# A pair's accumulators summed in mid-pair, the recurrence's elementwise work issued over three chunks, and the last two gate blocks made plain

## The chip, the cores and the metric

The kernel runs on one core of a Trainium2 chip. The metric is the time of one execution in device microseconds; it is given as the median of three runs. A profile is one execution taken by the hardware profiler, and its times count from the start of its span.

## The reference

A decoder layer of width 2048 on 256 tokens in float32. Two token mixers, a retention and a gated linear recurrence (RG-LRU), run on the same normalized input; their projections are weighted by sigmoid gates and added. Then come a cross attention to 256 memory tokens, a gated feed-forward network and a norm. Cut to the part that the change touches:

```python
hn = rmsnorm(h, norm_mix_w[l])
q, k, v, g_ret, xr, yr, g_a, g_b = jnp.split(hn @ w_in[l], offsets, axis=-1)
...
ret = head_groupnorm(chunkwise_retention(q, k, v), ret_gn_w[l]).reshape(b, s, D_RET_V)
ret_out = jax.nn.silu(g_ret) * ret
xr = causal_dwconv(xr, rnn_conv_w[l], rnn_conv_b[l])
hr = rg_lru(xr, rg_w_a[l], rg_b_a[l], rg_w_x[l], rg_b_x[l], rg_lambda[l])
rnn_out = jax.nn.gelu(yr) * hr
merged = (jax.nn.sigmoid(g_a) * (ret_out @ w_proj_ret[l])
          + jax.nn.sigmoid(g_b) * (rnn_out @ w_proj_rnn[l]))
h = h + merged @ w_mix_out[l]
```

`xr`, `yr`, `g_a`, `g_b`, and the two projections are each 2048 columns wide.

## The kernel before

**Weights.** All weights pass once through SBUF, in chunks of 512 rows by 512 columns (1 MB, a tile of 128x2048 float32 that holds 4 row tiles). `weight_plan` lists the matrix products in the order of the program, `weight_units` turns them into chunks ("units"), and `prefetch` brings each chunk in ahead of its use: a load on SP's queue (L259), then `hi`, the chunk cast to the fast matmul format by ACT (L280), and `lo`, the rest, subtracted by DVE (L281). Five buffers hold raw chunks, three each hold `hi` and `lo`, and chunks are prepared two units ahead. The left operand is split in the same way, and each product takes three matmuls: high by hi, low by hi, high by lo.

**Blocks.** `gemm_t` (L318, matmuls at L340) gives a transposed block of 512 columns; `gemm_n` (L354, matmuls at L350 to L352) gives a plain one, four units of 24 matmuls of 128x512, 96 in all, in one accumulator. Accumulators are PSUM tiles of two banks from a pool with three buffers, so at most three are alive.

**Pairs.** `pair_products` (L364, matmuls at L378, L380, L381) computes two neighbouring blocks of 512 columns together, with one product less out of eight on the first half of the contraction (a Strassen-like scheme of seven products q1 to q7); the second half is done plainly by four units `p`. The order is `PAIR_UNITS`: q1, p, q3, p, q5, q2, q6, p, p, q7, q4. A q unit has 12 matmuls and a p unit 24: 180 in place of the 192 of two plain blocks. Some q units need sums of weight chunks. These are formed by accumulating loads on POOL's queue (L261, "add" in the table: three to a pair) or by DVE (L285); q6 uses the sum as it stands. A pair has 10 loads and 11 splits, two plain blocks have 8 of each. The left operand's sums (`ss`) come from `sums` (L443): four small DVE subtractions and a split.

A pair uses three accumulators, all that there are: `xz` (halves x and z), `yu` and `rw`. x is begun by q1, and later by q6 and q7; z by q5; r by q3 and the first two p units; w by those p units; y by q2 and the last two p units; u by those and q4. After each unit `pair_products` calls `out`, which `pair_out` (L420 to L440) defines for the pairs of this study: two SBUF tiles o0 and o1 gather the parts of x, z, yu and rw:

```python
            elif kind == "q7":
                act.copy(o0[:, 1, :], x)
                dve.tensor_tensor(out=o1[:, 1, :], in0=o1[:, 1, :], in1=x, op=ALU.subtract)
            elif kind == "q4":
                dve.tensor_tensor(out=o1, in0=o1, in1=rw, op=ALU.add)
                dve.tensor_tensor(out=o0, in0=o0, in1=yu, op=ALU.add)
```

In the trace these are L433 and L434 (q7) and L436 and L437 (q4); q1's copy is L427, q5's is L429, q6's subtraction is L431. `pair_add` (L396) is another `out`, used later in the kernel.

**Order.** The loops are fully unrolled. A tile framework orders the instructions of each engine by priorities and puts in the semaphores; `later(n, fn)` holds back `fn` until n + 1 further units have been issued.

**Stages.** After retention: four times `recurrent(b)` (an XR and a YR block by `gemm_t`, then `recur(b)` after the next unit), two GA pairs, two GB pairs, two pairs of `w_proj_ret`, four plain blocks of `w_proj_rnn`, then the output projection. `recur` (L807 to L841) has the gates' small matmuls, six ACT functions a tile, DVE work at L825, L826, L830 and L831, four scans (L833) and two products (L839), stored to DRAM by POOL's queue. Retention's and the recurrence's results lie in DRAM in eight rows each (`Kept`); `ret[i]` or `rnn[i]` brings a row back through POOL's queue (L680), splits it (L496 and L497 for ret, L499 and L500 for rnn), and for ret[0] to ret[3] forms its sums. Rows 0 to 3 of ret are asked for during the second GB pair, rows 4 to 7 when `w_proj_ret`'s first p units use them. `sum_x(i)` (L873), i = 0 to 3, forms the sums of the input x; all four are asked for from block b = 2 on. The gates' tanh (L906) works on o0 and o1 and leaves them in `sig`; `gated` (L910) multiplies the projections by them.

Of the kernel before, what the change touches and what calls it, by code (L numbers as in the profile page):

```python
# [28 lines left out]
KC = 4  # L29
# [34 lines left out]
def weight_plan():  # L64

    w0 = "w_in"
    plan = []
    for g in range(2):
        for c in (O_Q, O_K):
            plan += [(w0, 0, NT, c + g * BW), (w0, 0, NT, O_V + g * 1024 + (c == O_K) * BW)]  # L70
        plan += [(w0, 0, NT, O_G + g * 1024 + b * BW) for b in range(2)]
    for b in range(4):
        plan += [(w0, 0, NT, c + b * BW) for c in (O_XR, O_YR)]
    for w, c in ((w0, O_GA), (w0, O_GB), ("w_proj_ret", 0)):
        plan += [(w, 0, NT, c + b * BW, c + (b + 1) * BW) for b in (0, 2)]
# [73 lines left out]
def hybrid_layer(  # L149
# [143 lines left out]
    def later(n, fn):  # L293

        pending.append((step[0] + n + 1, fn))
# [125 lines left out]
    def pair_out(w, st, ss, c0):  # L421

        o0, o1 = (big([P, 2, BW], s="o") for _ in range(2))

        def out(kind, x, z, yu, rw):
            if kind == "q1":
                act.copy(o0[:, 0, :], x)  # L427
            elif kind == "q5":
                act.copy(o1, z[:, None, :].to_broadcast([P, 2, BW]))  # L429
            elif kind == "q6":  # L430
                dve.tensor_tensor(out=o1[:, 0, :], in0=o1[:, 0, :], in1=x, op=ALU.subtract)  # L431
            elif kind == "q7":
                act.copy(o0[:, 1, :], x)  # L433
                dve.tensor_tensor(out=o1[:, 1, :], in0=o1[:, 1, :], in1=x, op=ALU.subtract)  # L434
            elif kind == "q4":
                dve.tensor_tensor(out=o1, in0=o1, in1=rw, op=ALU.add)  # L436
                dve.tensor_tensor(out=o0, in0=o0, in1=yu, op=ALU.add)  # L437

        pair_products(w, 0, st, ss, c0, c0 + BW, out)
        return o0, o1  # L440
# [368 lines left out]
    def recur(b, rgw, xr, gl):  # L809
        aa, tt_, ti = big([P, 4, S], s="aa"), big([P, 4, S], s="tt"), big([P, 4, S], s="ti")  # L810
        for j in range(4):
            t = 4 * b + j
            c1 = slice(t, t + 1)
            gp = small()
            for i in range(2):
                pe.matmul(gp[:, i, :], rgw[:, i, j, :], xr[:, j, :], start=True, stop=True)
            tr = tp.tile([P, S], F32, tag="tr", bufs=2, name=nm("tr"))
            act.activation(tr, gp[:, 0, :], AF.Tanh, scale=0.5, bias=half_ba[:, c1])
            act.activation(ti[:, j, :], gp[:, 1, :], AF.Tanh, scale=0.5, bias=half_bx[:, c1])
            act.activation(aa[:, j, :], tr, AF.Exp, scale=neg_half_c[:, c1], bias=neg_half_c[:, c1])  # L820
            act.activation(tt_[:, j, :], tr, AF.Tanh, scale=half_c[:, c1], bias=half_c[:, c1])
        for pr in range(2):
            cs = slice(2 * pr, 2 * pr + 2)
            a2 = tmp("a2")
            dve.tensor_tensor(out=a2, in0=aa[:, cs, :], in1=aa[:, cs, :], op=ALU.mult)  # L825
            dve.scalar_tensor_tensor(  # L826
                out=tt_[:, cs, :], in0=a2, scalar=1.0, in1=tt_[:, cs, :], op0=ALU.add, op1=ALU.mult
            )
        act.activation(tt_, tt_, AF.Sqrt, scale=0.25)
        dve.scalar_tensor_tensor(out=ti, in0=ti, scalar=1.0, in1=xr, op0=ALU.add, op1=ALU.mult)  # L830
        dve.tensor_tensor(out=ti, in0=ti, in1=tt_, op=ALU.mult)  # L831
        for j in range(4):
            dve.tensor_tensor_scan(  # L833
                out=xr[:, j, :], data0=aa[:, j, :], data1=ti[:, j, :], initial=0.0, op0=ALU.mult, op1=ALU.add
            )
        for pr in range(2):
            o = tmp("rn")
            cs = slice(2 * pr, 2 * pr + 2)
            dve.tensor_tensor(out=o, in0=xr[:, cs, :], in1=gl[:, cs, :], op=ALU.mult)  # L839
            rnn.store(o)  # L840

    def recurrent(b):
        rgw = big([P, 2, 4, P], s="rgw")
        for i, src in enumerate((rg_w_a, rg_w_x)):
            sp.dma_start(out=rgw[:, i], in_=src[0, 4 * b : 4 * b + 4].rearrange("g i j -> i g j"))
        xr = big([P, 4, S], s="xr")
        for pr, a in enumerate(gemm_t("w_in", 0, xs, NT, O_XR + b * BW)):
            z = scaled(a, "xz")
            for j in range(2):
                t = 4 * b + 2 * pr + j  # L850
                y = xr[:, 2 * pr + j, :]
                act.activation(y, z[:, j, :], AF.Identity, scale=p_cw(3, t), bias=p_cb(t))
                for s in range(1, 4):
                    dve.scalar_tensor_tensor(
                        out=y[:, s:S], in0=z[:, j, 0 : S - s], scalar=p_cw(3 - s, t), in1=y[:, s:S],
                        op0=ALU.mult, op1=ALU.add,
                    )
        gl = big([P, 4, S], s="gl")
        for pr, a in enumerate(gemm_t("w_in", 0, xs, NT, O_YR + b * BW)):
            y = scaled(a, "yz")  # L860
            y2, th = tmp("y2"), tmp("yt")
            act.activation(y2, y, AF.Square)
            dve.tensor_scalar(out=y2, in0=y2, scalar1=0.044715 * K0, scalar2=K0, op0=ALU.mult, op1=ALU.add)
            dve.tensor_tensor(out=y2, in0=y2, in1=y, op=ALU.mult)
# [4 lines left out]
        later(0, lambda a=(b, rgw, xr, gl): recur(*a))  # L869

    xs_sums = []

    def sum_x(i):  # L873

        t = tmp("xt")
        pool.dma_start(out=t, in_=x_t[:, 2 * i : 2 * i + 2, :])
        for j in range(2):
            act.activation(t[:, j, :], t[:, j, :], AF.Identity, scale=p_mix(2 * i + j))
        xs_sums.append(sums(t))
# [11 lines left out]
                merged.append(split_pair(t, 0.5))  # L891

    for b in range(4):
        if b == 2:
            for i in range(KC):
                later(2 + 3 * i, lambda i=i: sum_x(i))
        recurrent(b)
    sig = []
    for c in (O_GA, O_GB):
        for b in (0, 2):  # L900
            if c == O_GB and b == 2:
                for i in range(KC):
                    later(3 + 2 * i, lambda i=i: ret[i])
            for t in pair_out("w_in", xs, xs_sums, c + b * BW):
                for tt in range(2):
                    act.activation(t[:, tt, :], t[:, tt, :], AF.Tanh, scale=half_rs0[:, tt : tt + 1])  # L906
                sig.append(t)
# [288 lines left out]
```

## Time and profile before

| | us |
|---|---|
| time, median of 3 runs | 2064.91 (2062.55 to 2066.58) |
| profiled execution | 2064.81 |
| its span | 2063.0 |
| TensorE clock granted, mean | 0.994 |

| stage | first matmul of its blocks, us |
|---|---|
| YR blocks, b = 0 to 3 | 308.66, 360.26, 410.53, 458.91 |
| GA pairs | 482.89 and 537.14 |
| GB pairs | 582.16 and 627.16 |
| w_proj_ret pairs | 670.78 and 723.82 |
| w_proj_rnn, first block | 766.41 |

The page's engines are PE (matmul), PEld (its weight load, which overlaps), DVE, ACT, POOL and SP. In a row of instructions, `out<-in` are the program's names with the buffer numbers left out, `[1.98 <-DVE o L434]` is the idle time of the engine before it and the instruction that ended it, and x counts instructions. A busy time of PE contains matmuls that ran at a lower clock; the distance between the starts of two matmuls shows both.

### The profile page before, as it was taken

The page shows a single profiled execution, that of the slowest core. Times are in us where ns is not written, and L with a number is a line of the kernel's source. Part 1 is how long each engine was busy: PE and PEld are TensorE (multiplying, and loading weights), DVE is VectorE, ACT ScalarE, POOL GpSimd, SP SyncE. Part 2 cuts the span into 40 slices and gives each one's busy share as a digit, 9 for nine tenths or more (in the row PEclk, how much of TensorE's full clock was granted, in tenths as well). Part 3 has the DMA queues.
Part 4 walks back from the last instruction along what each step waited for, and adds up shares of the span by engine and source line. Part 5 has one row for each costly group of instructions (what it writes and reads, how often), then busy time and mean ns, then how long its engine had stood idle before and what let it go on. Part 6 is the DMA issues. An engine that isn't in the chain of part 4 may idle for free.

```text
span 2063.0 us, 25251 instructions
## 1 busy us (share of the span) xinstructions
PE 2021.7 (98%) x10364; PEld 1723.4 (84%) x10364; DVE 1454.1 (70%) x1491; ACT 1095.8 (53%) x1102; POOL 59.5 (3%) x84
## 2 busy tenths in 40 slices
PE   9999999998999899999999999999999999999998
PEld 8888888887777778888888888888878888788887
DVE  6746657889768686676555557578778687776775
ACT  6445447677557554456444455455555555454543
POOL 0000000001001000000000000000000000000000
PEclk9999999999999999999999999999999999999999
DMA  9555554555888785686445457555568555685552
GB/s 372 205 207 184 184 194 168 206 211 152 256 246 283 215 252 204 211 288 225 174 170 183 161 174 230 184 185 190 196 184 270 191 202 192 167 275 212 185 203 82
DMA packets 70820, 426.80 MB, mean 207 GB/s; under 512 B 7984, under 2 KB 12720, under 8 KB 22448
## 3 DMA queue, kind: packets, MB, share of 16 engines
q1 hardware_dynamic: 61120, 375.37, 49.6%
q0 software_dynamic: 8064, 47.19, 10.9%
q10 hardware_dynamic: 1520, 2.63, 0.4%
q8 instruction: 81, 1.33, 0.2%
q14 instruction: 35, 0.29, 0.0%
HBM read 418.87 MB, written 6.29 MB: 206 GB/s over the span
## 4 chain that ended last, share of the span: by engine, by line
PE 61%; DVE 3%; DMA 2%; ACT 1%; issue 1%; POOL 0%; POOLq 0%; ACTq 0%; DVEq 0%
PE acc L340 32%; PE acc L350 5%; PE acc L352 5%; PE acc L351 5%; PE acc L381 4%; PE acc L380 4%; PE acc L378 4%; DMA raw<-in_wall 2%; DVE lo L281 2%; PE sm L466 1%; ACT hi L280 1%; PE sm L478 1%; DVE fv L1072 0%; DVE s L500 0%; DVE raw L285 0%
## 5 line engine op out<-in xcount | busy, mean ns | idle before, releaser
L281 DVE TENSOR_TENSOR lo<-raw,hi 128x2048 fp32r<-128x2048 f32 (+1 forms) x396 | 895.5, 2268 | 477.2 <-ACT hi L280 469.4
L280 ACT CAST hi<-raw 128x2048 fp32r<-128x2048 f32 (+1 forms) x394 | 747.2, 1900 | 689.3 <-issue 172.0
L340 PE MATMUL acc<-s,hi 128*128 128x512 f32 x2688 | 641.5, 391 | 2.8 <-DVE xz L489 1.5
L340 PEld LDWEIGHTS acc<-s,hi 128*128 128x128 f32 x2688 | 496.6, 188 | 101.7 <-issue 3.7
L340 PEld LDWEIGHTS acc<-s,lo 128*128 128x128 f32 x2688 | 343.2, 191 | 13.5 <-DVE lo L281 2.3
L340 PE MATMUL acc<-s,lo 128*128 128x256 f32 x2688 | 350.6, 284 | 1.7 <-DVE lo L281 1.7
L350 PE MATMUL acc<-hi,s 128*128 128x512 f32 (+1 forms) x760 | 292.6, 385 | 1.2 <-DVE o L434 1.2
L352 PE MATMUL acc<-lo,s 128*128 128x512 f32 (+1 forms) x760 | 291.2, 383 | 0.0
L351 PE MATMUL acc<-hi,s 128*128 128x512 f32 (+1 forms) x760 | 290.9, 383 | 0.0
L378 PE MATMUL acc<-hi,s 128*128 128x512 f32 x528 | 210.1, 398 | 18.0 <-DVE o L434 11.8
L381 PE MATMUL acc<-lo,s 128*128 128x512 f32 x528 | 209.0, 396 | 2.1 <-DVE lo L281 1.9
L380 PE MATMUL acc<-hi,s 128*128 128x512 f32 x528 | 208.9, 396 | 1.6 <-DVE s L497 1.6
L350 PEld LDWEIGHTS acc<-hi,s 128*128 128x128 f32 x760 | 142.9, 188 | 28.6 <-DVE o L434 1.6
L352 PEld LDWEIGHTS acc<-lo,s 128*128 128x128 f32 x760 | 142.8, 188 | 28.5 <-DVE lo L281 0.2
L351 PEld LDWEIGHTS acc<-hi,s 128*128 128x128 f32 x760 | 143.0, 188 | 27.2 <-DVE s L500 0.2
L378 PEld LDWEIGHTS acc<-hi,s 128*128 128x128 f32 x528 | 100.8, 191 | 42.5 <-DVE o L434 13.9
L381 PEld LDWEIGHTS acc<-lo,s 128*128 128x128 f32 x528 | 100.8, 191 | 25.7 <-DVE lo L281 4.6
L380 PEld LDWEIGHTS acc<-hi,s 128*128 128x128 f32 x528 | 100.9, 191 | 23.7 <-DVE s L497 2.3
L488 ACT COPY c<-acc 128x512 f32<-128x512 f32 x84 | 48.1, 579 | 91.9 <-PE acc L340 91.9
L381 PE MATMUL acc<-lo,ss 128*128 128x512 f32 x192 | 75.7, 394 | 2.7 <-DVE lo L281 2.7
L378 PE MATMUL acc<-hi,ss 128*128 128x512 f32 x192 | 76.1, 396 | 1.4 <-ACT o L429 1.3
L380 PE MATMUL acc<-hi,ss 128*128 128x512 f32 x192 | 75.4, 393 | 0.0
(227 smaller groups left out, 1293.1 us busy)
## 6 DMA issues: line engine op xcount, KB each, us to landing
raw<-in_wall SPq DMA_DIRECT2D x341, 1024.0 KB, 4.9
raw<-in_wall POOLq DMA_DIRECT2D x36, 1024.0 KB, 9.6
raw<-in_wall SPq DMA_DIRECT2D x5, 512.0 KB, 7.5
nat<-in_x ACTq DMA_DIRECT2D x4, 512.0 KB, 10.4
ret<-hd POOLq DMA_DIRECT2D x8, 256.0 KB, 6.8
rnn<-rn POOLq DMA_DIRECT2D x8, 256.0 KB, 2.6
kt<-ret POOLq DMA_DIRECT2D x8, 256.0 KB, 11.0
kt<-rnn POOLq DMA_DIRECT2D x8, 256.0 KB, 7.3
```

The lines of the kernel that those rows point to most:

```text
L280: act.copy(hi[:, a:b], raw[:, a:b])
L281: dve.tensor_tensor(out=lo[:, a:b], in0=raw[:, a:b], in1=hi[:, a:b].bitcast(F32), op=ALU.subtract)
L340: pe.matmul(a, part, sx, start=k == 0 and t == 0, stop=k == nk - 1 and t == 0, skip_group_check=True)
L350: pe.matmul(o, h, hi, start=start, stop=False)
L351: pe.matmul(o, l, hi, start=False, stop=False)
L352: pe.matmul(o, h, lo, start=False, stop=stop)
L378: pe.matmul(o[0], h, hi, start=o[1] not in begun, stop=False, skip_group_check=True)
L380: pe.matmul(o[0], l, hi, start=False, stop=False, skip_group_check=True)
L381: pe.matmul(o[0], h, lo, start=False, stop=kk == KC - 1, skip_group_check=True)
L466: pe.matmul(o, a, b, start=start and i == 0, stop=stop and i == 2, skip_group_check=True)
L478: pe.transpose(t[:, j, tt * P : (tt + 1) * P], rows[:, tt, k + j * P : k + (j + 1) * P], ident)
L488: act.copy(c, a[:, :, S:BW])
```

## The change

Three parts.

1. In `pair_out`, the addition of rw to o1 moves from the end of the pair (after q4) to `later(1)` after q5, that is after q2.
2. In `recur`, the elementwise work behind the gates' functions is cut in three functions, issued one, two and three units later. `sum_x` is asked for in blocks b = 1 (i = 0, 1) and b = 2 (i = 2, 3), every fourth unit from the third on.
3. Blocks 2 and 3 of GB become two plain blocks by `gemm_n`, whose tanh reads the accumulator and writes a tile "sig". Rows 0 to 3 of ret are asked for there, two to a block; rows 4 to 7 after the first two units of `w_proj_ret`'s first pair; the rows of rnn one unit earlier than before in its second pair.

```diff
-    for w, c in ((w0, O_GA), (w0, O_GB), ("w_proj_ret", 0)):
-        plan += [(w, 0, NT, c + b * BW, c + (b + 1) * BW) for b in (0, 2)]
+    for w, c, pairs in ((w0, O_GA, (0, 2)), (w0, O_GB, (0,)), ("w_proj_ret", 0, (0, 2))):
+        plan += [(w, 0, NT, c + b * BW, c + (b + 1) * BW) for b in pairs]
+        if len(pairs) == 1:
+            plan += [(w, 0, NT, c + b * BW) for b in (2, 3)]
...
                 act.copy(o1, z[:, None, :].to_broadcast([P, 2, BW]))
+                later(1, lambda: dve.tensor_tensor(out=o1, in0=o1, in1=rw, op=ALU.add))
...
             elif kind == "q4":
-                dve.tensor_tensor(out=o1, in0=o1, in1=rw, op=ALU.add)
                 dve.tensor_tensor(out=o0, in0=o0, in1=yu, op=ALU.add)
...
+        def weigh():
+            for pr in range(2):
...
+            act.activation(tt_, tt_, AF.Sqrt, scale=0.25)
+
+        def drive():
+            dve.scalar_tensor_tensor(out=ti, in0=ti, scalar=1.0, in1=xr, op0=ALU.add, op1=ALU.mult)
+            dve.tensor_tensor(out=ti, in0=ti, in1=tt_, op=ALU.mult)
+
+        def scan():
+            for j in range(4):
...
+        for n, fn in enumerate((weigh, drive, scan)):
+            later(n, fn)
...
     for b in range(4):
-        if b == 2:
-            for i in range(KC):
-                later(2 + 3 * i, lambda i=i: sum_x(i))
+        if b in (1, 2):
+            for i in range(2):
+                later(2 + 4 * i, lambda i=2 * b - 2 + i: sum_x(i))
         recurrent(b)
     sig = []
-    for c in (O_GA, O_GB):
-        for b in (0, 2):
-            if c == O_GB and b == 2:
-                for i in range(KC):
-                    later(3 + 2 * i, lambda i=i: ret[i])
...
+    def gate(t, a):
+        for tt in range(2):
+            act.activation(t[:, tt, :], a[:, tt, :], AF.Tanh, scale=half_rs0[:, tt : tt + 1])
+        sig.append(t)
+
+    for c, b in ((O_GA, 0), (O_GA, 2), (O_GB, 0)):
+        for t in pair_out("w_in", xs, xs_sums, c + b * BW):
+            gate(t, t)
+    for b in (2, 3):
+        for i in range(2):
+            later(2 * i, lambda i=2 * b - 4 + i: ret[i])
+        gate(big([P, 2, BW], s="sig"), gemm_n("w_in", 0, xs, NT, O_GB + b * BW))
+    for i in range(KC):
+        later(i // 2, lambda i=i: ret[KC + i])
...
-                later(8 + i, lambda i=i: rnn[i])
+                later(7 + i, lambda i=i: rnn[i])
```

More of the change, by code (lines that the diff above doesn't have):

```diff
@@ L821, in recur @@
             act.activation(tt_[:, j, :], tr, AF.Tanh, scale=half_c[:, c1], bias=half_c[:, c1])
[L822 to L840, printed above, removed]
+        def weigh():
+            for pr in range(2):
+                cs = slice(2 * pr, 2 * pr + 2)
+                a2 = tmp("a2")
+                dve.tensor_tensor(out=a2, in0=aa[:, cs, :], in1=aa[:, cs, :], op=ALU.mult)
+                dve.scalar_tensor_tensor(
+                    out=tt_[:, cs, :], in0=a2, scalar=1.0, in1=tt_[:, cs, :], op0=ALU.add, op1=ALU.mult
+                )
+            act.activation(tt_, tt_, AF.Sqrt, scale=0.25)
[4 more added lines that the diff above has]
+            for j in range(4):
+                dve.tensor_tensor_scan(
+                    out=xr[:, j, :], data0=aa[:, j, :], data1=ti[:, j, :], initial=0.0, op0=ALU.mult, op1=ALU.add
+                )
+            for pr in range(2):
+                o = tmp("rn")
+                cs = slice(2 * pr, 2 * pr + 2)
+                dve.tensor_tensor(out=o, in0=xr[:, cs, :], in1=gl[:, cs, :], op=ALU.mult)
+                rnn.store(o)
+        for n, fn in enumerate((weigh, drive, scan)):
+            later(n, fn)
     def recurrent(b):
@@ L868, in recurrent @@
             )
-        later(0, lambda a=(b, rgw, xr, gl): recur(*a))
+        later(0, lambda: recur(b, rgw, xr, gl))
     xs_sums = []
@@ L893, in hybrid_layer @@
     for b in range(4):
-        if b == 2:
-            for i in range(KC):
-                later(2 + 3 * i, lambda i=i: sum_x(i))
+        if b in (1, 2):
+            for i in range(2):
+                later(2 + 4 * i, lambda i=2 * b - 2 + i: sum_x(i))
         recurrent(b)
     sig = []
-    for c in (O_GA, O_GB):
-        for b in (0, 2):
-            if c == O_GB and b == 2:
-                for i in range(KC):
-                    later(3 + 2 * i, lambda i=i: ret[i])
[L904 to L907, printed above, removed]
+    def gate(t, a):
[11 more added lines that the diff above has]
+        later(i // 2, lambda i=i: ret[KC + i])
     def gated(t, z):
```

## Prediction

> **What bounds the kernel now.** I read the page first for who is busy, then the windows of the six stretches that the change touches, then the timeline of PE, DVE and ACT at each place where PE stands still. The profiled execution took 2064.81 us, 1.8 us more than its span, and lies 0.1 us below the median of 2064.91; the sum below is made against 2064.81.
>
> ```profile
> span 2063.0 us, 25251 instructions
> PE 2021.7 (98%) x10364; PEld 1723.4 (84%) x10364; DVE 1454.1 (70%) x1491; ACT 1095.8 (53%) x1102; POOL 59.5 (3%) x84
> L378 PE MATMUL acc<-hi,s 128*128 128x512 f32 x528 | 210.1, 398 | 18.0 <-DVE o L434 11.8
> ```
>
> PE is the bound, so what counts is where PE isn't fed. The pairs' first matmul line, L378, has the longest idle time of the page's groups of PE, and two thirds of it is put down to one DVE instruction, the subtraction of L434. A busy PE can also be a slow PE, so I take distances between matmul starts instead of busy time. The next rows are windows: start:end, length, then busy time (x instructions) of PE, PEld, DVE, ACT and POOL, the granted clock, DMA share and GB/s. Each of the first five runs from the last matmul of one pair to the last of the next.
>
> ```profile
> 533.56:579.79 46.23, 43.03 (x182) 34.77 (x180) 32.48 (x23) 26.66 (x19) 4.37 (x6) 0.96 0.80 240
> 579.79:624.79 45.00, 43.00 (x182) 34.76 (x180) 30.68 (x17) 25.27 (x18) 2.14 (x4) 0.96 0.78 227
> 624.79:668.20 43.41, 41.41 (x181) 33.63 (x180) 35.12 (x25) 29.42 (x26) 6.98 (x11) 1.00 0.89 273
> 668.20:720.99 52.79, 45.98 (x182) 36.20 (x180) 32.75 (x21) 27.32 (x22) 3.82 (x5) 0.90 0.72 219
> 720.99:764.83 43.84, 41.38 (x182) 33.63 (x180) 36.64 (x25) 26.71 (x22) 2.57 (x3) 1.00 0.84 252
> 586.61:602.93 16.32, 16.32 (x74) 13.51 (x72) 9.84 (x5) 8.13 (x5) 0.85 (x1) 1.00 0.46 141
> 96.42:118.18 21.76, 21.76 (x97) 18.02 (x96) 10.58 (x6) 8.83 (x7) 0.00 (x0) 1.00 0.56 194
> ```
>
> An undisturbed stretch inside a pair makes 72 steps in 16.32 us, and an undisturbed plain block 96 in 21.76: 0.2267 us a step in both. A pair's 180 steps are thus worth 40.80 us. The five windows exceed that by 5.43, 4.20, 2.61, 11.99 and 3.04 us: 27.27 us that are no arithmetic. DVE has 8 to 20 us free in each, and yet PE waits for it. Why, the boundary at 580 shows (start, us, engine and line; in brackets the idle time before and who ended it):
>
> ```profile
> 579.79 0.39 PE L381 MATMUL acc<-lo,s 128*128 128x512 f32 x1
> 582.16 0.50 PE L378 MATMUL acc<-hi,s 128*128 128x512 f32 x1 [1.98 <-DVE o L434]
> 583.15 0.63 PE L378 MATMUL acc<-hi,s 128*128 128x512 f32 x1
> 583.57 0.63 PE L380 MATMUL acc<-hi,s 128*128 128x512 f32 x1
> 586.61 0.39 PE L378 MATMUL acc<-hi,s 128*128 128x512 f32 x1
> ```
>
> ```profile
> 579.22 2.29 DVE L281 TENSOR_TENSOR lo<-raw,hi 128x2048 fp32r<-128x2048 f32 x1 [0.42 <-ACT hi L280]
> 581.42 0.68 DVE L434 TENSOR_TENSOR o<-o,acc 128x512 f32<-128x512 f32 x1
> 582.02 1.21 DVE L437 TENSOR_TENSOR o<-o,acc 128x1024 f32<-128x1024 f32 x1
> 583.15 1.21 DVE L436 TENSOR_TENSOR o<-o,acc 128x1024 f32<-128x1024 f32 x1
> ```
>
> Three accumulators xz, yu, rw are all there are, so q1 of the next pair must take one that the pair before has emptied. It gets xz, which q7's subtraction empties last, and that stands on DVE behind a lo of 2.29 us. The idle time is not all: after it the matmuls start 0.42 apart (583.15, 583.57) instead of 0.2267. From 579.79 to 586.61 lie 13 steps, worth 2.95 us, in 6.82: the boundary costs 3.87 us. The rest of this pair loses 4.20 - 3.87 = 0.33 us, mostly in the wait before q6, and I let every remaining pair keep it.
>
> **The change, part by part: the rw add moves from q4 to the end of q2.** The amount of work is unchanged, 1.21 us on DVE by the row of L436. In the changed program's order, rw is given back in mid-pair, and the next pair's xz takes that buffer; the buffer that L434's successor empties goes to the next pair's first p unit, 12 matmuls or 2.72 us later. So each boundary is weighed by whether the subtraction ends within 2.72 us of the time at which q1 can start, which is one step after the last matmul.
>
> ```profile
> 537.14 0.50 PE L378 MATMUL acc<-hi,s 128*128 128x512 f32 x1 [3.19 <-DVE o L434]
> 541.81 0.40 PE L380 MATMUL acc<-hi,s 128*128 128x512 f32 x1
> 674.99 0.39 PE L381 MATMUL acc<-lo,s 128*128 128x512 f32 x1
> 678.37 0.80 PE L378 MATMUL acc<-hi,s 128*128 128x512 f32 x1 [2.99 <-ACT s L496]
> 680.78 0.80 PE L380 MATMUL acc<-hi,s 128*128 128x512 f32 x1 [1.61 <-DVE s L497]
> 685.65 0.40 PE L380 MATMUL acc<-hi,s 128*128 128x512 f32 x1
> 766.41 0.50 PE L350 MATMUL acc<-hi,s 128*128 128x512 f32 x1 [1.20 <-DVE o L434]
> ```
>
> ```profile
> 536.40 0.68 DVE L434 TENSOR_TENSOR o<-o,acc 128x512 f32<-128x512 f32 x1
> 680.04 2.49 DVE L497 TENSOR_TENSOR s<-kt,s 128x512 fp32r<-128x512 f32 x4
> 723.08 0.68 DVE L434 TENSOR_TENSOR o<-o,acc 128x512 f32<-128x512 f32 x1
> ```
>
> - First to second GA pair: 533.56 to 541.81 is 8.25 us for 14 steps (3.17), a loss of 5.08. The p unit now wants the buffer at 533.56 + 0.23 + 2.72 = 536.51; L434 ends at 537.08. Some 0.65 us stays. Gain 4.43.
> - GA to GB: wanted at 582.74, emptied at 582.10. Gain the whole 3.87.
> - First to second proj_ret pair: wanted at 723.94, emptied at 723.76. Gain 3.04 - 0.33 = 2.71. Only 0.18 us of cover: if that is gone, what exceeds it comes back as a wait.
> - proj_ret to proj_rnn: L350's first start is 764.83 + 1.58, of which 0.23 is a step, and the start after it is 0.11 late. The plain block needs one buffer, and rw's is free. Gain 1.46.
>
> The added work in mid-pair stands on DVE between two lo's. In the first GA pair, the tightest since the recurrence's scans come before it, the rows are:
>
> ```profile
> 511.57 6.69 DVE L281 TENSOR_TENSOR lo<-raw,hi 128x2048 fp32r<-128x2048 f32 x3
> 518.17 0.68 DVE L431 TENSOR_TENSOR o<-o,acc 128x512 f32<-128x512 f32 x1
> 519.66 2.29 DVE L281 TENSOR_TENSOR lo<-raw,hi 128x2048 fp32r<-128x2048 f32 x1 [0.80 <-ACT hi L280]
> ```
>
> The third lo there ends at 518.2 and would end at 519.5. It belongs to the second p unit after q6: q6's first lo matmul is at 513.91 (quoted below), its other steps take some 4 us at the slow spacing, and the p unit between has 24 steps (5.4), so it is wanted at about 523.3. I cost the add at 0. Its cover is 3.8 us there and DVE's free time of 8 to 20 us a pair elsewhere; without that cover every pair would pay up to 1.21.
>
> **The second GB pair becomes two plain blocks.** 192 matmuls instead of 180: +12 x 0.2267 = +2.72 us. Gone are the pair's 2.61 us of loss, its three accumulating loads on POOL's queue and three of its 11 splits, so ACT, DVE and DMA have more room, and rows 0 to 3 of ret, which move into these blocks, have 24 matmuls to a unit to hide behind. The boundary behind it falls too: 668.20 to 674.99 is 6.79 us for 12 steps (2.72), 4.07 lost; tanh reads the plain block's buffer itself, and two others are free for q1 and the p unit. Gain 2.61 + 4.07 - 2.72 = 3.96.
>
> **Rows 4 to 7 of ret.** From 674.99 to 685.65 there are 14 steps (3.17) in 10.66: 7.49 us lost. The first p unit wants s of row 4 on the spot, and ACT makes it too late:
>
> ```profile
> 671.89 2.56 ACT L906 ACTIVATE o<-o,half_rs 128x512 f32<-128x512 f32 x4 [1.59 <-DVE o L437]
> 675.42 0.58 ACT L427 COPY o<-acc 128x512 f32<-128x512 f32 x1 [0.96 <-PE acc L381]
> 675.90 1.90 ACT L280 CAST hi<-raw 128x2048 fp32r<-128x2048 f32 x1
> 677.70 2.18 ACT L496 CAST s<-kt 128x512 fp32r<-128x512 f32 x4
> ```
>
> Afterwards ACT's order from the start T of q1 is: one hi (1.90), two tanh (half of 2.56), the copy of q1 (0.58), then row 4's cast (2.18 for four, some 0.6 alone). It is done at T + 4.4, and its lo on DVE (2.49 for four) at T + 5.0. The p unit wants the cast at T + 2.72 and the lo a step later, at T + 2.95, so 2.1 us are lost; rows 6 and 7 are wanted two units later and are in time. Whether the clock falls after that wait I can't know: at 582 it did, while the windows from 624.79 and 720.99, which begin with the same kind of wait, have a clock of 1.00. Ends 2.1 and 3.7 (with 1.6 of slow steps: 3.87 lost at 580 less the wait itself, 582.16 - 579.79 - 0.23); I take 3.0 between them. Gain 4.49.
>
> The Trainium skill (TensorE: Matmul & The Clock Gate, "What's actually happening") has the clock halved after an idle window of about 3.4 us, and its table in "Why this matters for your kernels" asks only that gaps stay below some 3 us. This trace halves it after 1.98 us, so the rule doesn't hold as a threshold here; by it the wait would cost 2.1, and the time be 0.9 us lower.
>
> **The recurrence and sum_x.** The recurrence is issued in three steps and sum_x one block earlier; nothing is added. PE stands still near them at these places:
>
> ```profile
> 364.89 0.98 PE L340 MATMUL acc<-s,lo 128*128 128x256 f32 x6 [1.67 <-DVE lo L281]
> 468.89 1.85 PE L340 MATMUL acc<-s,hi 128*128 128x512 f32 x7 [1.47 <-DVE xz L489]
> 513.91 0.50 PE L381 MATMUL acc<-lo,ss 128*128 128x512 f32 x1 [2.72 <-DVE lo L281]
> ```
>
> In the first GA pair the changed program has the scans in the same place of DVE's order, so the third stays. In the gemm_t blocks some lo's now stand between or ahead of the scans, and row 3's sums no longer lie before 468.89. That could take both stalls away (-3.1) or make two like them where sums now stand (+3.1). I take 0.
>
> **Sum.** Gains 4.43 + 3.87 + 2.71 + 1.46 + 3.96 + 4.49 = 20.92 us. 2064.81 - 20.92 = 2043.9; I say 2044. Its own range: the recurrence's 3.1 to both sides, 0.9 of the clock, and 2 us of boundary covers that could run out: 2039 to 2050.
>
> **The rivals.**
> - *The wait only moves on.* L434's successor ends later than now, since DVE's lo's shift with PE, and the first p unit waits as q1 did. For it: covers of -0.57, 0.64 and 0.18 us. Against it: on DVE, the 1.21 of L436 is out of the way at the end. Then the three pair boundaries' 11.0 us are not gained: 2055.
> - *Slower: DVE becomes the bound in mid-pair.* The rw add holds back the lo behind it in each of the five pairs that remain, with the price of the only such wait on record, 2.72 at 513.91, five times 13.6; and the boundaries get nothing, as the subtraction stands behind the same late lo's. 2054.9 + 13.6 = 2068.5, and with 1.6 of slow steps on each, 2076.5. It decides from the point where the add comes more than 3.8 us too late. Against it: 31 to 37 us of DVE work in windows of 43 to 53.
> - *No net change.* Half the boundary gain is lost, row 4's wait stays at 7.49, and the gemm_t stages lose 3.1 with as much again in slow steps: 2044 + 5.5 + 4.5 + 6.2 = 2060, and a little more makes it 2064.
>
> **How the numbers follow.** Chances: forecast 0.66, the wait moving on 0.20, no net change 0.05, slower 0.09. A measurement of this kernel can tell 0.2% (4.1 us) from no change. Faster is the first two, 0.86. The range reaches from 2038 over the second case's 2055 to 2057; it leaves out the last two cases and a little of the tails.
>
> **What would show it.** Right: L378's 11.8 us put down to L434 falls below 2; windows of 180 steps take 41 to 42 us; no 0.42 spacing at 580; row 4's wait of about 2 us some 2.7 us after proj_ret's q1. Wrong: idle time of L378 put down to the subtraction of q7 or to lo at the second unit, the wait before it now on the first p unit; new stalls on L340 between 300 and 490; a mid-pair wait for lo in pairs after the first.

## The result, and the profile after

| | before | changed | ratio, 95% interval |
|---|---|---|---|
| first timing, median of 4 runs each, us | 2063.73 (2061.62 to 2066.58) | 2042.67 (2039.33 to 2046.23) | 0.9897 (0.9875 to 0.9919) |
| timed again, medians of 7 and 4 runs, us | 2064.62 (2063.89 to 2069.70) | 2041.42 (2040.21 to 2041.58) | 0.9882 (0.9867 to 0.9897) |
| profiled execution, us | 2064.81 | 2039.33 | |
| first matmul of w_proj_rnn, us into the span | 766.41 | 742.03 | |

The change takes 21 us off by the first timing and 23 us by the second. In the trace, 24.4 us are won by the time w_proj_rnn starts. The page of the changed kernel, its span, its engines, and its group of the pairs' first matmul line (L378 before, L380 now):

```profile
span 2037.5 us, 25259 instructions
PE 2015.9 (99%) x10376; PEld 1721.5 (84%) x10376; DVE 1441.1 (71%) x1483; ACT 1087.1 (53%) x1096; POOL 56.8 (3%) x81
L380 PE MATMUL acc<-hi,s 128*128 128x512 f32 x484 | 189.5, 392 | 4.5 <-ACT hi L282 3.2
```

The idle time of this line fell from 18.0 to 4.5 us, and the subtraction of q7 (L437 now) isn't the first releaser any more: in the whole trace no matmul of this line waits for it, and one weight load does, for 0.3 us. PE has 12 more matmuls and is busy 5.8 us less: fewer matmuls ran at the lower clock (its mean is 0.998, it was 0.994). The windows from last matmul to last matmul, as before (start:end, length, busy time and count of PE, PEld, DVE, ACT, POOL, clock, DMA share, GB/s); the third is the two plain blocks:

```profile
531.64:572.89 41.25, 41.24 (x182) 33.63 (x180) 32.18 (x23) 25.18 (x18) 3.88 (x6) 1.00 0.87 264
572.89:614.01 41.12, 41.10 (x181) 33.69 (x180) 32.38 (x21) 27.26 (x22) 4.62 (x7) 1.00 0.88 267
614.01:657.53 43.52, 43.52 (x193) 36.04 (x192) 24.53 (x15) 20.60 (x17) 3.08 (x5) 1.00 0.74 262
657.53:700.69 43.16, 41.66 (x181) 33.63 (x180) 29.56 (x18) 25.95 (x20) 3.38 (x5) 1.00 0.72 229
700.69:741.80 41.11, 41.10 (x181) 33.70 (x180) 35.42 (x24) 26.15 (x21) 2.12 (x3) 1.00 0.86 253
```

A pair is worth 40.80 us, and three of the four now take 0.31 to 0.45 us more, with the clock at 1.00. The plain blocks take exactly their 192 steps of 0.2267. One window, the first of w_proj_ret, still loses 2.36. PE's timeline at the places of the prediction:

```profile
363.81 0.39 PE L342 MATMUL acc<-s,lo 128*128 128x256 f32 x1 [0.57 <-DVE lo L283]
412.71 0.50 PE L342 MATMUL acc<-s,hi 128*128 128x512 f32 x1 [0.66 <-DVE xz L491]
505.98 0.50 PE L380 MATMUL acc<-hi,ss 128*128 128x512 f32 x1 [1.29 <-ACT o L431]
512.15 0.80 PE L383 MATMUL acc<-lo,ss 128*128 128x512 f32 x1 [2.70 <-DVE lo L283]
...
534.59 0.49 PE L380 MATMUL acc<-hi,s 128*128 128x512 f32 x1
...
572.89 0.39 PE L383 MATMUL acc<-lo,s 128*128 128x512 f32 x1
573.11 0.39 PE L380 MATMUL acc<-hi,s 128*128 128x512 f32 x1
575.83 0.39 PE L380 MATMUL acc<-hi,s 128*128 128x512 f32 x1
...
661.85 0.51 PE L380 MATMUL acc<-hi,s 128*128 128x512 f32 x1 [1.21 <-ACT s L498]
662.63 0.50 PE L382 MATMUL acc<-hi,s 128*128 128x512 f32 x1 [0.27 <-DVE s L499]
662.96 0.39 PE L383 MATMUL acc<-lo,s 128*128 128x512 f32 x1
```

```profile
533.84 0.68 DVE L437 TENSOR_TENSOR o<-o,acc 128x512 f32<-128x512 f32 x1
574.53 0.68 DVE L437 TENSOR_TENSOR o<-o,acc 128x512 f32<-128x512 f32 x1
702.33 0.68 DVE L437 TENSOR_TENSOR o<-o,acc 128x512 f32<-128x512 f32 x1
```

From the GA pair to the GB pair PE goes on after one step, 572.89 to 573.11, while DVE is not yet at the subtraction: it ends at 575.21, 0.62 us ahead of the p unit at 575.83 that takes the buffer. At the boundary before it ends at 534.52, 0.07 ahead of the p unit at 534.59. That is the new order of who waits for whom: the subtraction is as late as before (it ends 2.32 us after the GA pair's last matmul, and ended 2.31 after it), and nobody needs it yet.

### The profile page after: what moved, and what is told of

The parts are those of the page before. It is cut to its first block, busy times and chain, and to the rows that moved or that the text cites. A ratio compares the mean times of both kernels' runs of the same rounds, so it can differ in the third digit from the quotient of the medians.

```text
span 2037.5 us, 25259 instructions
## 1 busy us (share of the span) xinstructions
PE 2015.9 (99%) x10376; PEld 1721.5 (84%) x10376; DVE 1441.1 (71%) x1483; ACT 1087.1 (53%) x1096; POOL 56.8 (3%) x81
## 4 chain that ended last, share of the span: by engine, by line
PE 89%; DVE 4%; ACT 3%; DMA 2%; issue 1%; POOL 0%; POOLq 0%; SPq 0%; ACTq 0%; DVEq 0%
PE acc L342 43%; PE acc L352 9%; PE acc L354 9%; PE acc L353 9%; PE acc L383 6%; PE acc L380 5%; PE acc L382 5%; DVE lo L283 2%; DMA raw<-in_wall 2%; PE sm L468 2%; ACT hi L282 1%; PE sm L480 1%; DMA xt<-in_mem_t 0%; DVE fv L1088 0%; ACT tt L823 0%
## 5 line engine op out<-in xcount | busy, mean ns | idle before, releaser
L352 PE MATMUL acc<-hi,s 128*128 128x512 f32 (+1 forms) x824 | 317.3, 386 | 0.0
L354 PE MATMUL acc<-lo,s 128*128 128x512 f32 (+1 forms) x824 | 316.1, 384 | 0.0
L353 PE MATMUL acc<-hi,s 128*128 128x512 f32 (+1 forms) x824 | 315.9, 383 | 0.0
L380 PE MATMUL acc<-hi,s 128*128 128x512 f32 x484 | 189.5, 392 | 4.5 <-ACT hi L282 3.2
L383 PE MATMUL acc<-lo,s 128*128 128x512 f32 x484 | 189.2, 391 | 0.8 <-DVE lo L283 0.5
L382 PE MATMUL acc<-hi,s 128*128 128x512 f32 x484 | 189.2, 391 | 0.3 <-DVE s L499 0.3
L380 PEld LDWEIGHTS acc<-hi,s 128*128 128x128 f32 x484 | 90.9, 188 | 24.8 <-ACT hi L282 4.7
L383 PE MATMUL acc<-lo,ss 128*128 128x512 f32 x176 | 69.5, 395 | 2.7 <-DVE lo L283 2.7
L380 PE MATMUL acc<-hi,ss 128*128 128x512 f32 x176 | 69.7, 396 | 1.3 <-ACT o L431 1.3
L382 PE MATMUL acc<-hi,ss 128*128 128x512 f32 x176 | 69.0, 392 | 0.0
```

The lines of the kernel that those rows point to most:

```text
L352: pe.matmul(o, h, hi, start=start, stop=False)
L353: pe.matmul(o, l, hi, start=False, stop=False)
L354: pe.matmul(o, h, lo, start=False, stop=stop)
L380: pe.matmul(o[0], h, hi, start=o[1] not in begun, stop=False, skip_group_check=True)
L382: pe.matmul(o[0], l, hi, start=False, stop=False, skip_group_check=True)
L383: pe.matmul(o[0], h, lo, start=False, stop=kk == KC - 1, skip_group_check=True)
```

## The experiments

The traces' total is a poor scale for parts of some us. From w_proj_rnn's first matmul to the last, the programs do the same work, and yet this stretch took between 1286.6 and 1291.0 us in the traces of this study. So the parts are compared by the time from the 1001st matmul (199.40 us into the span before) to w_proj_rnn's first: 567.01 us before, and 24.4 less in the changed kernel. The table gives this "stretch" beside the times. A stretch is read from one trace, and the same kernel's differ: by 0.5 us in the two traces of the changed kernel, by 1.7 in the two of the last version. Part of it is the clock. After some waits the matmuls start 0.42 to 0.43 us apart for a while, and such a group of slow steps costs some 1.6 us or more; the last column is what they cost in the stretch: the sum of what the distance between two starts exceeds 0.2267 us by, over groups of three or more such matmuls of the pairs and plain blocks, waits left out. It is 8.3 us for the kernel before and 1.5 for the changed one.

| kernel | median, us | before beside it | ratio, 95% interval | stretch, us against before | slow steps in it, us |
|---|---|---|---|---|---|
| rw add moved alone | 2047.02 | 2064.49 | 0.9920 (0.9906 to 0.9935) | -17.7 | 4.0 |
| plain blocks and rows alone | 2058.85 | 2064.49 | 0.9975 (0.9965 to 0.9984) | -3.1 | 9.4 |
| both of these | 2042.57 | 2064.49 | 0.9897 (0.9880 to 0.9913) | -22.6 | 0 |
| recurrence and sum_x alone | 2063.71 | 2064.49 | 0.9994 (0.9984 to 1.0004) | -0.2 | 7.7 |
| changed, two DVE passes more | 2046.67 | 2065.78 | 0.9911 (0.9894 to 0.9928) | -18.3 | 2.9 |
| changed, four DVE passes more | 2067.36 | 2065.78 | 1.0004 (0.9992 to 1.0015) | +2.7 | 8.8 |
| changed, rows 4 and 5 early | 2039.22 | 2065.78 | 0.9872 (0.9855 to 0.9889) | -26.4 | 1.6 |
| changed, last scans after q7's and q4's work | 2045.13 | 2065.78 | 0.9896 (0.9877 to 0.9915) | -19.0 | 2.6 |
| changed, last scans between q7's and q4's lo | 2043.28 | 2063.93 | 0.9897 (0.9883 to 0.9912) | -21.8 | 2.8 |
| changed, second GB pair kept, rows 4 and 5 early | 2038.02 | 2063.93 | 0.9875 (0.9858 to 0.9891) | -27.4 | 1.6 |
| the same again | 2039.12 | 2064.62 | 0.9873 (0.9857 to 0.9890) | -25.7 | 0 |
| changed, again | 2041.42 | 2064.62 | 0.9882 (0.9867 to 0.9897) | -23.9 | 1.6 |

### The rw add alone

The kernel before, with this edit and nothing else:

```diff
                 act.copy(o1, z[:, None, :].to_broadcast([P, 2, BW]))
+                later(1, lambda: dve.tensor_tensor(out=o1, in0=o1, in1=rw, op=ALU.add))
...
             elif kind == "q4":
-                dve.tensor_tensor(out=o1, in0=o1, in1=rw, op=ALU.add)
```

> The kernel before with the first part of the change alone: rw is added to o1 after q2 instead of after q4; all six pairs stay, and the recurrence and the rows are asked for as before. Theory (the buffer rotation was the wait): the idle time of L378 put down to q7's subtraction, 11.8 us, goes to about 0, and with the slow steps behind it the boundaries give back 5.1 + 3.9 + 2.3 + 4.1 + 2.7 + 1.5 = 19.5 us, so a profiled execution of about 2045; the wait for row 4 of ret stays near 7 us. Rival (the wait moves to the first p unit): new idle time at the first p units, at least half of it back, 2054 or more.

Measured: 2047.0 us, span 2045.0. No boundary has a wait for q7's subtraction of over 0.3 us any more; what is left between the GB and the proj_ret pairs is ACT's row 4:

```profile
665.53 0.75 PE L378 MATMUL acc<-hi,s 128*128 128x512 f32 x1 [4.90 <-ACT s L496]
666.90 0.79 PE L380 MATMUL acc<-hi,s 128*128 128x512 f32 x1 [0.62 <-DVE s L497]
```

ACT starts this row's cast 7.1 us after the pair's first matmul (657.75 to 664.86), much as before (670.78 to 677.70, 6.9 us). But q1 now runs at the full clock and starts its last matmul 2.49 us after its first instead of 4.21, so PE waits 4.90 us for the row instead of 2.99, and 2.6 us of slow steps follow instead of 2.1. Nearly two of the 19.5 us expected went there. Moving the wait along is thus real for this row, and not for the accumulators. The buffer rotation was the cause of the waits at the boundaries.

### The plain blocks and rows alone

The kernel before with the third part of the change, rw added after q4.

> The kernel before with the third part alone: the second GB pair as two plain blocks, rows of ret and rnn asked for as in the change; rw is added after q4 as before. Theory: the boundary into the first proj_ret pair goes (4.1), row 4's wait falls from 7.5 to about 2 (5.4), the added matmuls cost 2.7, the boundaries behind pairs stay: 2064.8 - 6.8 = 2058. Rival (the plain blocks carry most of the change's gain): 2050 or less.

Measured: 2058.9 us. The boundaries behind pairs keep their waits, also the one in front of the first plain block:

```profile
583.21 0.50 PE L380 MATMUL acc<-hi,s 128*128 128x512 f32 x1 [1.98 <-DVE o L436]
628.18 0.80 PE L352 MATMUL acc<-hi,s 128*128 128x512 f32 x1 [1.98 <-DVE o L436]
720.36 0.80 PE L380 MATMUL acc<-hi,s 128*128 128x512 f32 x1 [1.98 <-DVE o L436]
```

The stretch gained 3.1 us, not 6.8. After the waits at 628.18 and 720.36 the matmuls start 0.43 apart, which the same boundaries were spared in the kernel before (clock 1.00 in its windows from 624.79 and 720.99). They do so too after the waits for row 4, 1.21 us at 677.50 and 0.28 at 678.28; the changed kernel has the same two waits and no slow steps after them. Each of the three groups costs 1.6 us, together more than the 3.7 that are missing.

### Both, and the recurrence alone

Two kernels: the change without its second part, and the second part alone on the kernel before.

> The change without its second part: recurrence in one piece and sum_x asked for in block 2 as before. Theory: the second part is worth only the two waits in the gemm_t blocks, between 1 and 3 us, so 2040 to 2043 in the profile, and the stalls of 1.67 and 1.47 us at L340 in blocks YR 1 and YR 3 are there again. Rival (the second part does more): 2045 or more.

> The kernel before with the second part alone: the recurrence's elementwise work in three steps and sum_x one block earlier. Theory: the waits at L340 in YR 1 and YR 3 shrink to under 1 us each, one new wait in YR 2; 1 to 3 us gained, 2062 to 2064. The first GA pair's waits of 1.3 and 2.7 us stay. Rival: nothing or a loss, 2065 to 2068.

The change without the second part has the stalls of blocks YR 1 and YR 3 again, and a wait at the first boundary:

```profile
365.07 0.50 PE L342 MATMUL acc<-s,lo 128*128 128x256 f32 x2 [1.66 <-DVE lo L283]
469.10 0.47 PE L342 MATMUL acc<-s,hi 128*128 128x512 f32 x1 [1.50 <-DVE xz L491]
536.46 0.50 PE L380 MATMUL acc<-hi,s 128*128 128x512 f32 x1 [0.85 <-DVE o L437]
```

Its median can't be told from the changed kernel's; in the stretch it is 1.8 us behind it, and 3.3 if slow steps aren't counted: it waits the same 2.71 us before q6, at 514.11, and no slow steps follow. The second part alone shrinks the same stalls as the changed kernel (to 0.58 us at 363.91, and 0.67 at 412.84), and its first GA pair ends 3.0 us earlier than before (530.59 against 533.56), 1.6 of them because no slow steps follow the wait before q6 here either. But then:

```profile
535.55 0.80 PE L378 MATMUL acc<-hi,s 128*128 128x512 f32 x1 [4.58 <-DVE o L434]
```

The wait at the boundary grew from 3.19 to 4.58 us, 2.8 us of slow steps followed instead of 1.6, and by the second boundary 0.6 us of the 3.0 are left. A gain ahead of a wait that is set by another engine is given back at the wait: the second part is worth 0.2 us by itself, and 1.8 beside the other two. The parts don't add in the stretch, where 17.7 + 3.1 + 0.2 is 21.0 and all three together give 24.4; but 2.9 of these 3.4 us are slow steps, so the clock is most of that difference.

### More work at the moved add

To measure the cover of the moved add, DVE passes over o1 that change nothing were put behind it, 1.2 us each, two or four to a pair:

```diff
-                later(1, lambda: dve.tensor_tensor(out=o1, in0=o1, in1=rw, op=ALU.add))
+
+                def rw_in():
+                    dve.tensor_tensor(out=o1, in0=o1, in1=rw, op=ALU.add)
+                    for _ in range(2):
+                        dve.tensor_tensor(out=o1, in0=o1, in1=o1, op=ALU.max)
+
+                later(1, rw_in)
```

> The changed kernel with two more DVE passes over o1 (its maximum with itself, 1.2 us each) right behind the moved rw add in each pair. Theory (the add is hidden by the time that the lo behind it has in hand, 3.5 us in the second pair, 562.1 - 558.6): 2.4 us more in each of five pairs cost nothing, time within 1 us of the changed kernel's. Rival (DVE is near to being the bound in mid-pair): 5 x 1 to 2.4 us, 5 to 12 us more.

> The same with four more passes, 4.8 us in each pair. Theory: more than the 3.5 us in hand, so the second p unit after q6 waits about 0.8 us for its lo in each of the five pairs, 2 to 5 us more than the changed kernel. Rival: nothing again (the cover is larger than thought), or more than 12 us (each pass counts in full).

Both cost more than expected: in the stretch, two passes 6.1 us and four 27.1 us, or 5.4 us a pair for 4.8 us of work; without the slow steps, 4.7 and 19.9. For four passes the rival, by which each counts in full, was nearer than the theory. With two passes, the first GA pair carries 3.3 us of it (PE, then DVE, then DVE at the same place in the changed kernel):

```profile
529.28 0.80 PE L380 MATMUL acc<-hi,ss 128*128 128x512 f32 x1 [2.19 <-DVE o L440]
```

```profile
526.33 2.29 DVE L283 TENSOR_TENSOR lo<-raw,hi 128x2048 fp32r<-128x2048 f32 x1 [3.59 <-ACT hi L282]
528.54 0.68 DVE L440 TENSOR_TENSOR o<-o,acc 128x512 f32<-128x512 f32 x1
```

```profile
517.55 0.68 DVE L434 TENSOR_TENSOR o<-o,acc 128x512 f32<-128x512 f32 x1
518.15 2.29 DVE L283 TENSOR_TENSOR lo<-raw,hi 128x2048 fp32r<-128x2048 f32 x1
525.69 2.29 DVE L283 TENSOR_TENSOR lo<-raw,hi 128x2048 fp32r<-128x2048 f32 x1 [4.32 <-ACT hi L282]
```

L440 is q6's subtraction (L434 in the changed kernel), and the PE row is the start of q7 (the scheduler has put two of q4's matmuls ahead of it). q7 writes on into the accumulator x that q6's subtraction has to read first. That subtraction works on o1, behind rw's add and the passes, and the scheduler has put it behind q4's lo, ahead of which it stood in the changed kernel. The hi of that lo is late in both kernels: ACT begins it at 524.40 after 7.32 us without work, until its load has landed, and at 523.75 in the changed one. DVE was idle for 3.59 us just ahead of this lo: here it isn't the amount of DVE work that costs, but who stands behind whom. With four passes this happens in later pairs too, together with a wait for q4's lo, which PE now wants ahead of q7 and for whose hi DVE itself waits 2.73 us:

```profile
577.14 0.50 PE L383 MATMUL acc<-lo,s 128*128 128x512 f32 x1 [1.16 <-DVE lo L283]
579.00 0.67 PE L380 MATMUL acc<-hi,ss 128*128 128x512 f32 x1 [0.90 <-DVE o L440]
```

The wait for q7's subtraction (L443 here) comes back as well, now on the next pair's first p unit, where the prediction's first rival, the wait that only moves on, expected it:

```profile
540.68 0.50 PE L380 MATMUL acc<-hi,s 128*128 128x512 f32 x1 [3.12 <-DVE o L443]
```

### The waits that are left

In the changed kernel, ACT makes row 4's cast (L498) behind two tanh and q1's copy:

```profile
659.55 1.26 ACT L912 ACTIVATE sig<-acc,half_rs 128x512 f32<-128x512 f32 x2
660.70 0.58 ACT L429 COPY o<-acc 128x512 f32<-128x512 f32 x1
661.16 1.16 ACT L498 CAST s<-kt 128x512 fp32r<-128x512 f32 x2
```

The rows' loads can't be what holds it up: the last of the eight landed at 612.44. So rows 4 and 5 of ret are asked for in the second plain block's last unit:

```diff
             later(2 * i, lambda i=2 * b - 4 + i: ret[i])
+        if b == 3:
+            later(3, lambda: ret[4])
+            later(3, lambda: ret[5])
...
-    for i in range(KC):
+    for i in range(2, KC):
         later(i // 2, lambda i=i: ret[KC + i])
```

> The changed kernel, with rows 4 and 5 of ret asked for in the last unit of the second plain block instead of after q1 of the first proj_ret pair. Theory (ACT's order made row 4's cast late): the waits of 1.6 and 0.8 us at the first p unit go, 2.0 us less than the changed kernel in the profile. Rival (another wait, for the buffer or for rows 6 and 7, takes their place): less than 1 us.

Measured: the waits at the first p unit are gone, and the stretch is 2.0 us shorter than the changed kernel's, as expected. The times, 2039.22 us here, can't tell a difference of this size.

The last recurrence's scans, moved back in the first GA pair; `(0, 7, 8)` is the first of two tries, `(0, 5, 5)` the second:

```diff
-        for n, fn in enumerate((weigh, drive, scan)):
+        for n, fn in zip((0, 1, 2) if b < 3 else (0, 7, 8), (weigh, drive, scan)):
             later(n, fn)
```

> The changed kernel, with the last recurrence's second and third step issued eight and nine units after its gates instead of two and three, so that in the first GA pair its scans and products stand behind q5's, q6's and the p units' lo's, and its two stores behind q4's accumulating load. Theory (the scans are what makes q6's lo late there, 2.86 us of wait and the slow steps behind it): this wait goes, 3 to 5 us less than the changed kernel, 2033 to 2036 in a profile. Rival (q6's lo is late because of its load or its hi): the wait stays above 2 us and the time within 1 us of the changed kernel's.

> The changed kernel with rows 4 and 5 of ret asked for one block earlier, and with the last recurrence's second and third step issued six and seven units after its gates, so that scans and products stand in DVE's order between q7's and q4's lo, in the time in which DVE waited for ACT's hi. Theory (order of DVE's work alone decides): the waits before q6 go and few come back at q7 and q4, 3 to 5 us less than with the rows alone; to the first w_proj_rnn block 28 to 31 us less than the kernel before. Rival (any place in the first GA pair costs the same, since accumulating loads and rows stand behind it on POOL's queue): 22 to 26 us less, as in the changed kernel or worse.

As run, the second kernel has not got the edit of the rows, and both steps are issued six units after the gates; so it stands against the changed kernel. In both, the wait of 2.70 us before q6 is gone and the recurrence's last steps are thus its cause. The first GA pair becomes 3.9 and 3.6 us shorter, from its first matmul to its last, and yet the stretch is longer in both, by 5.4 and 2.7 us. The second, PE, DVE and POOL:

```profile
505.64 0.50 PE L383 MATMUL acc<-lo,s 128*128 128x512 f32 x1 [0.57 <-DVE lo L283]
534.75 0.80 PE L380 MATMUL acc<-hi,s 128*128 128x512 f32 x1 [2.78 <-DVE o L437]
```

```profile
531.20 0.29 DVE L451 TENSOR_TENSOR sm<-kt 128x128 f32<-128x128 f32 x1 [1.88 <-DMA kt<-ret]
```

```profile
508.77 0.89 POOL L682 DMA_DIRECT2D kt<-ret  x1
522.03 1.11 POOL L675 DMA_DIRECT2D rnn<-rn  x2 [12.37 <-DVE rn L847]
523.14 1.11 POOL L682 DMA_DIRECT2D kt<-ret  x2
```

The rows of ret that the scheduler brings in early stand on POOL's queue behind the recurrence's two stores. With the scans later, the stores wait until 522.03, the rows are issued behind them, DVE waits 1.88 us for a row in order to form its sums, and behind those sums stand a lo and q7's subtraction, which the p unit of the next pair now lacks for 2.78 us. In the first try, the rows got between two accumulating loads of the next pair: the last of these, issued at 553.12, let ACT begin its hi only at 569.02 (in the changed kernel, one issued at 553.02 did at 565.84), and PE waited at 570.98:

```profile
548.38 1.40 POOL L682 DMA_DIRECT2D kt<-ret  x2
553.12 0.90 POOL L263 DMA_DIRECT2D raw<-in_wall  x1 [3.34 <-DVE lo L283]
```

```profile
570.98 0.50 PE L380 MATMUL acc<-hi,s 128*128 128x512 f32 x1 [1.71 <-ACT hi L282]
```

The theory of the second try failed, and its rival is what the traces show: what is gained in the first GA pair is lost again behind it. How much of that the order on POOL's queue costs is read from these rows alone: a version in which the stores or the rows leave POOL's queue wasn't tried.

### The second GB pair kept, and rows 4 and 5 early

With rw added in mid-pair, nothing in the traces so far asks for the plain blocks' room except row 4. So that pair is kept, with the weight plan of before, and rows 4 and 5 are asked for in its last unit:

```diff
-    for c, b in ((O_GA, 0), (O_GA, 2), (O_GB, 0)):
+    for c, b in ((O_GA, 0), (O_GA, 2), (O_GB, 0), (O_GB, 2)):
+        if c == O_GB and b == 2:
+            for i in range(KC):
+                later(3 + 2 * i, lambda i=i: ret[i])
+            for i in range(2):
+                later(10, lambda i=i: ret[KC + i])
         for t in pair_out("w_in", xs, xs_sums, c + b * BW):
             gate(t, t)
-    for b in (2, 3):
...
-    for i in range(KC):
+    for i in range(2, KC):
         later(i // 2, lambda i=i: ret[KC + i])
```

> The changed kernel with the second GB pair kept as a pair (180 matmuls instead of 192), its rows of ret asked for as before, and rows 4 and 5 asked for in this pair's last unit. Theory (with rw added in mid-pair and rows early, the plain blocks only cost their 12 matmuls): 2.7 less and 0.3 more than the changed kernel with early rows, 4.5 us less than the changed kernel in the trace up to the first w_proj_rnn block, 29 us less than the kernel before. Rival (the plain blocks' room on ACT, DVE and POOL's queue was needed): new waits in this pair or for row 4, no gain or a loss of some us against the changed kernel.

> The changed kernel itself, timed again beside the next. By the traces up to the first w_proj_rnn block it stands 24.5 us below the kernel before; its first timing gave 21.1. Theory (the traces tell the change, the rest is scatter between executions): 21 to 25 us below the kernel before.

> The second GB pair kept and rows 4 and 5 asked for early, timed again beside the changed kernel. Theory: 2 to 3 us less than the changed kernel, 25 to 28 us below the kernel before. Rival: no difference from the changed kernel that five rounds can tell.

Measured: 2038.0 us, and in the second timing, beside the changed kernel, 2039.12 (2038.57 to 2039.70) against 2041.42 (2040.21 to 2041.58). These four runs each don't overlap, though the intervals of the two ratios do; a lead of 2.3 us is likely, and not settled. The stretch is 3.0 and 1.8 us shorter than the changed kernel's in the two pairs of traces, less than the 4.5 expected, and 1.6 of the 1.8 are slow steps. In both traces two short waits for lo came in w_proj_ret's first pair, 0.17 and 0.49 us in the first, shown here, 0.77 and 0.87 in the second; no run here shows what brings them.

```profile
659.73 0.50 PE L381 MATMUL acc<-lo,s 128*128 128x512 f32 x1 [0.17 <-DVE lo L281]
696.20 0.50 PE L381 MATMUL acc<-lo,s 128*128 128x512 f32 x1 [0.49 <-DVE lo L281]
```

Against the changed kernel with early rows (stretch -26.4) it can't be told apart.

## Why the prediction was right, point by point

- **The boundaries.** Foreseen: the buffer is wanted one unit later, and the waits go except for 0.65 us at the first. They went: the windows of the second GA pair, the GB pair and the second proj_ret pair shrank by 4.98, 3.88 and 2.73 us, against 4.43, 3.87 and 2.71 in the sum, and the plain block of w_proj_rnn came 1.35 us nearer to the pair before it, as the wait there had been. The rw add alone shows it by itself. The 0.65 left over did not show in the changed kernel, where the subtraction was 0.07 us early, and does show, with 0.85, in the change without its second part: in a second trace of the changed kernel it is 0.23. No run here shows what decides it.
- **The plain blocks.** 2.72 us for 12 matmuls against 2.61 of loss: the window is 43.52 against 43.41. Right. That they take away the boundary into w_proj_ret is right as well, but so does the moved add by itself; the pair kept in the last version, 41.13 us in its window, shows that the 2.72 us needn't have been paid.
- **Row 4.** Foreseen 2.1 us of wait or 3.7 with slow steps, 3.0 taken; measured 2.04 (660.25 to 662.96 is 2.72 for three steps) and no slow steps. The wait was worked out right; that the slow steps stayed away is luck, as they follow the same two waits with the plain blocks alone. (They are worth 1.59 us by the steps at 583, as taken; the difference that the prediction gives for them comes to 1.73.) The gain of the window, 9.63, is 1.1 more than the 8.56 of the sum, nearly all by this term; the 0.33 that the sum let every pair keep is still there, as the window loses 2.36. ACT's order was the cause: the cast stands where the prediction put it, the load had landed long before, and asking for the rows one unit earlier removes the wait.
- **The recurrence.** Taken as 0 with 3.1 us to both sides; it is a gain: the first GA pair ends 1.92 us earlier than before. The stalls at 364.89 and 468.89 shrank and went, as the favourable end had them, and a new one of 0.66 came at 412.71, where sums now stand. The step that was off is this one: the ends were right, the value between them wasn't.
- **The rw add at no cost.** Its result held: no wait in mid-pair is put down to it. Its working did not. The 3.8 us were worked out from one lo, and DVE's free time, given as 8 to 20 us a pair, is 7.2 in the last window. The nearer limit is q6's subtraction, which must have read x before q7 writes to it, and which stands behind the add on the same tile. The price named for a lost cover, up to 1.21 us for the add, is near what the four passes cost, 27.1 us for twenty passes of 1.2, or 19.9 without slow steps; but it isn't paid evenly, as two passes cost 6.1 us over five pairs, 3.3 of it in one. The slower rival had the right kind of mechanism, DVE's order in mid-pair, with the wrong instruction and the wrong point at which it decides: 2.4 us of passes cost something, and the cover was put at 3.8.
- **The total.** 2044 forecast, 2042.7 and 2041.4 measured. Up to w_proj_rnn 24.4 us were won against 20.9: 1.9 from the recurrence, 0.55 at the first boundary, 1.1 at row 4. All three fell on the side of a gain. That the first timing still lies only 1.3 us from the forecast is in part luck: the timings, 21 and 23 us, scatter with the code behind w_proj_rnn's start.

## What to carry to other kernels

When an accumulator pool rotates, look which buffer the next user gets, and at which instant the last reader lets go of it; giving back a different buffer early can move a wait by a whole unit for no work at all. Ask of an operation that is hidden not how long its engine is idle, but which instructions are queued behind it and who has to have them next: the deadline may be a reader of the same accumulator and not the operand that one thinks of first. A gain ahead of a wait that another engine or queue sets is given back at that wait, so parts of a change are worth more or less together than alone. Count slow steps apart before parts are compared: a group of them can be as large as the part.

## What the runs showed of the hardware

- The clock fell to about half (0.51 from 583.2 to 586.2 us in the kernel before, the matmuls 0.42 to 0.43 us apart, for some 3.4 us) after waits far shorter than that: after 1.98 us at 582.16 in the kernel before and at all three places of 1.98 shown for the plain blocks alone. At 627.16 in the kernel before, a wait of 1.99 did not bring it. The same wait falls on either side at other places too. The 2.70 us before q6 brought it in the changed kernel, and the 2.71 at 514.11 of the change without its second part did not. The waits of 1.21 and 0.27 us at row 4 did not bring it in the changed kernel; after 1.21 and 0.28 with the plain blocks alone the matmuls from 679.72 to 682.70 start 0.43 apart. The Trainium skill (TensorE: Matmul & The Clock Gate, "What's actually happening") has a window of 3413 ns that runs free of the kernel, and the clock halved after at least one idle window. That the same wait brings the slow steps at one place and not at another agrees with it; that a wait of 1.98 us is enough doesn't agree with a full idle window.
- The same code takes different times in different executions: w_proj_rnn to the end 1286.6 to 1291.0 us. At 1522 us the changed kernel waits 0.31 us for a lo and the one with early rows 1.59, in the same instructions; both rows lie behind an accumulating load, whose landing differs: ACT, which waits for it, begins its hi 11.8 us after the issue in the one (1506.32 to 1518.16) and 13.5 in the other (1504.54 to 1518.00).
